# A decoder block with a dense expert stage: more first-layer blocks ahead of it, another DRAM layout for the gates, and a separate place for v's raw buffers

## The chip, the cores and the metric

The kernel runs on one core of one Trainium2 chip, in fp32. The metric is the device time of one execution in microseconds (us), lower is better. The kernel before took 3766.08 us (median of 3 runs, 3752.55 to 3779.93). The profile that is read here is one further execution, of 3775.4 us.

## What is computed

One decoder block over 1024 tokens of width 1024: two gated token mixers (a convolution module and an RWKV-7 scan), then PEER, a mixer that takes 128 experts per token (8 heads, top 16 of each) out of 16384. The change is in the part for PEER, which is in the reference:

```python
e = (i1 * PEER_NKEYS + i2).reshape(TOK_BLOCK, PEER_HEADS * K)      # 128 experts for each token
gate = jax.nn.softmax(best_s, axis=-1).reshape(TOK_BLOCK, PEER_HEADS * K)
u = expert_u[e]
act = jax.nn.gelu(jnp.einsum('td,ted->te', xb, u), approximate=False)
coef = (gate * act.astype(jnp.float32)).astype(xb.dtype)
return jnp.einsum('te,ted->td', coef, expert_v[e])
```

Before it stand the two mixers and the routing (query product and top-k), behind it a norm. None of them is edited.

## The kernel before

The tokens are worked in eight tiles of 128. PEER is done in two ways. Tiles 0, 1 and 2 **gather**: for each of the 128 experts of a token, one indirect DMA (line 1002, issued by POOL) brings 128 rows of 8 KB (the expert's u and v, 1 MB in all) into one of three `row` buffers; VectorE (DVE) takes the dot product with the token (line 1005), ScalarE (ACT) the Gelu and the gate (lines 1006 and 1007), and DVE adds the scaled v to the sum (line 997), which frees the buffer. Tile 0 is gathered before the dense stage, tiles 1 and 2 (256 gathers) beside it, two for each block. Tile 3 takes its activations by gathers ahead of it and the second layer densely.

Tiles 4 to 7 (512 tokens) are **dense**: all 16384 experts, as 128 blocks of 128, are multiplied out, and a gate that is zero for an expert that was not chosen picks the right ones. It has these stages.

- `spread_gates`: for 32 tokens at a time one-hot matrices are built on DVE, ACT and POOL (lines 1073 to 1084), and TensorE (PE) multiplies them (line 1085) into `gt`, whose entry for (expert inside a block, block, token) is the gate. `gt` has two buffers. Each of the 20 pieces goes to DRAM tensor `gd` by one DMA from ACT's queue (line 1089), but for blocks 0 to 7, which stay in two tiles in SBUF (`direct`).
- `u_stage`, the first layer of a block: two loads of 256 KB from `eut` (line 234, SP's queue), split into high and low fp32r parts on ACT and POOL (lines 224 and 225), 24 matmuls of 128x512 (lines 228 to 230), Gelu. It is run ahead of the dense stage for the blocks in `PRE` (56 of 128), and its 256 KB result `g1` is stored in DRAM (`gs`, line 1232) and loaded again (line 1129). These blocks run beside `spread_gates` and the gathers of tile 0.
- `dense`: 32 groups of four blocks. For each group one tile of gates, `gblk` (1.25 MB), is loaded from `gd` (line 1124), in two DMAs; for each block `u_stage` is run if the block is not in `PRE`, the activation is multiplied by the gate (line 1132) and split into `c`; then for each half of v's columns the four blocks' rows of v are loaded (`vraw`, 256 KB each, line 1149, three buffers), split into `vhi` and `vlo`, and 60 matmuls for five token tiles are added up (line 1159). So a group has 120 matmuls of the second layer, and 96 more where its blocks are not in `PRE`.

`PRE` holds every other group, 0, 2, ... 26. Groups 28 to 31 are not in it. These are called PRE groups and full groups below.

The order on each engine is set by a scheduler that works with its own estimate of times, from program order and priorities; on the chip each engine and each DMA queue then runs its instructions strictly in that order. SP issues all loads of the dense stage: an issue that waits holds back those behind it. The pools for `vhi`, `vlo` and `vraw` (`vb`) and for `c` (`cb`) are opened after `spread_gates` has closed its own, and lie where those were.

Of the kernel before, what the change touches and what calls it, by code (L numbers as in the profile page):

```python
# [10 lines left out]
F32 = mybir.dt.float32  # L11
# [9 lines left out]
P = 128  # L21
# [10 lines left out]
GT = 32  # L32
# [3 lines left out]
WD = 512 + XD  # L36
DT = list(range(4, 8)) + list(range(NGT, 4))
NG, NQ, GB, NB = WD // GT, 512 // GT, 4, 4
PRE = [b for b in range(128) if b // 4 % 2 == 0][:56]
NROW = 3  # L40
NV2 = 6
SOONER = 300
# [90 lines left out]
def body(tc, a, out):  # L133
    nc = tc.nc
    V, A, G, PE, SY = nc.vector, nc.scalar, nc.gpsimd, nc.tensor, nc.sync
# [9 lines left out]
    top = ExitStack()  # L145
    cp = pool(top, "cp")
    dr = pool(top, "dr", space=DRAM)
# [40 lines left out]
    zr = [dr.tile([P, 1 + T], F32, name=f"zr{j}") for j in range(14)]  # L188
    hd = [dr.tile([P, D], F32, name=f"hd{j}") for j in range(4)]
    xg = [dr.tile([P, D], F32, name=f"xg{j}") for j in range(4)]  # L190
    gd = dr.tile([NG, P, P, GT], F32, name="gd")
    gs = [dr.tile([P, 512], F32, name=f"gs{b}") for b in range(P)]
    sga = [[dr.tile([P, 512], F32, name=f"sga{j}_{h}") for h in range(2)] for j in range(16)]
    sil = [[dr.tile([P, 512], F32, name=f"sil{j}_{h}") for h in range(2)] for j in range(4)]
# [848 lines left out]
    def spread_gates(es, direct):  # L1043

        gtp = pool(es, "gtp", 2)
        sb = pool(es, "sg_", 2)
        ps_ = pool(es, "sgp", 2, PSUM)
        keys = ps_.tile([P, P], F32, name="keys", bufs=1)
        A.activation(keys, iota, AF.Copy)
        for s_, tt in sorted(enumerate(DT), key=lambda x: x[1]):  # L1050
            hf, tl = divmod(tt, 4)
            src = []
            for k in range(3):
                f = sb.tile([P, P], F32, name="gsrc", tag="gsrc")
                if k < 2:
                    ii = sb.tile([P, P], I32, name="gint", tag="gint")
                    V.tensor_single_scalar(ii, idx[hf][:, tl], 7 if k == 0 else 127,
                                           op=OP.logical_shift_right if k == 0 else OP.bitwise_and)
                    V.tensor_copy(f, ii)
                else:  # L1060
                    f = gate[1][:, tl] if hf else coef[0]
                pt = ps_.tile([P, P], F32, name="gtp")
                PE.transpose(pt, f, ident)
                ft = sb.tile([P, P], F32, name=f"gT{k}")
                A.activation(ft, pt, AF.Copy)
                src.append(ft)
            for g in range(P // GT):
                gt = gtp.tile([P, P, GT], F32, name="gt")
                for q in range(GT // 4):
                    pg = ps_.tile([P, 4, P], F32, name="pg", bufs=3)  # L1070
                    t0 = GT * g + 4 * q
                    o2 = sb.tile([P, 4, P], F32, name="o2h", bufs=3)
                    V.tensor_tensor(o2, src[1][:, t0:t0 + 4, None].to_broadcast([P, 4, P]),
                                    keys[:, None, :].to_broadcast([P, 4, P]), op=OP.is_equal)
                    o1 = sb.tile([P, 4, P], F32, name="o1h", bufs=3)
                    V.tensor_tensor(o1[:, :2], src[0][:, t0:t0 + 2, None].to_broadcast([P, 2, P]),
                                    keys[:, None, :].to_broadcast([P, 2, P]), op=OP.is_equal)
                    for x in range(4):
                        t = t0 + x
                        if x < 2:  # L1080
                            A.activation(o1[:, x], o1[:, x], AF.Copy, scale=src[2][:, t:t + 1])  # L1081
                        else:
                            (V if x == 2 else G).tensor_scalar(o1[:, x], keys if x == 2 else iota, src[0][:, t:t + 1], src[2][:, t:t + 1],
                                                               op0=OP.is_equal, op1=OP.mult)
                        PE.matmul(pg[:, x], o2[:, x], o1[:, x], start=True, stop=True)  # L1085
                    A.activation(gt[:, :, 4 * q:4 * q + 4], pg.rearrange("p t i -> p i t"), AF.Copy)
                for k, d in enumerate(direct):
                    A.activation(d[:, P // GT * s_ + g], gt[:, GB * k:GB * k + GB], AF.Copy)
                A.dma_start(gd[P // GT * s_ + g][:, GB * len(direct):], gt[:, GB * len(direct):])


    def u_stage(b, g1, x2, pu=None):
# [4 lines left out]
        A.activation(pu if g1 is None else g1, pu, AF.Gelu)  # L1097
        return pu

    def dense(es, x2, gp, hr, direct, gk1):  # L1100

        cb = pool(es, "cb")
        rows = gather_rows(gp, range(1, NGT), NROW, {}, pool(es, "rp", 1, PSUM))
        vb = pool(es, "vb", 2, side="right")
# [10 lines left out]
        for g0 in range(0, P, NB):  # L1115
            blks = range(g0, g0 + NB)
            cs = []
            for b in blks:
                if b < GB * len(direct):
                    gtile = direct[b // GB]  # L1120
                elif b % GB == 0:
                    gtile = gk[b // GB % 2].tile([P, NG, GB, GT], F32, name="gblk", tag="gblk")
                    for qs in (slice(0, NQ), slice(NQ, NG)):
                        SY.dma_start(gtile[:, qs].rearrange("p q b t -> p q (b t)"),  # L1124
                                     gd[qs, :, b:b + GB].rearrange("q p b t -> p q (b t)"))
                g1 = up.tile([P, 512], F32, name="g1")
                if b in PRE:
                    act = g1
                    SY.dma_start(g1, gs[b])
                else:  # L1130
                    act = u_stage(b, None, x2, bank())
                V.tensor_mul(g1.rearrange("p (q t) -> p q t", q=NQ), act.rearrange("p (q t) -> p q t", q=NQ), gtile[:, :NQ, b % GB])
                c2 = cb.tile([P, 2, WD], F32R, name="c2", bufs=NB + 1)
                split(c2[:, 0, :512], c2[:, 1, :512], g1)
                split(c2[:, 0, 512:].rearrange("p (q t) -> p q t", t=GT), c2[:, 1, 512:].rearrange("p (q t) -> p q t", t=GT),
                      gtile[:, NQ:, b % GB])
                cs.append(c2)
                if b == NB - 1:
                    for tt in range(NGT, 4):
                        hb[tt] = gp.tile([P, D], F32, name="hr3", tag="hr0")  # L1140
                        SY.dma_start(hb[tt], hd[tt])
                for _ in range(0 if b < NB - 1 else 2 * NB if b == NB - 1 else 2):
                    next(rows, None)
            for n in range(2):
                ns = slice(512 * n, 512 * n + 512)
                vs = []
                for b in blks:
                    raw = vb.tile([P, 512], F32, name="vraw", bufs=3)
                    SY.dma_start(raw, a["euv"][b * P:(b + 1) * P, D + 512 * n:D + 512 * n + 512])
                    hi = vb.tile([P, 512], F32R, name="vhi", bufs=NV2)  # L1150
                    lo = vb.tile([P, 512], F32R, name="vlo", bufs=NV2)
                    split(hi, lo, raw)
                    vs.append((hi, lo))
# [67 lines left out]
    with tc.high_priority(offset=LATER):  # L1221
        gather_coefs(gp, NGT, NEARLY, P)
        for _ in gather_rows(gp, [0], NROW, pace):
            pass
    gk1 = pool(top, "gk1", side="right")
    direct = [p.tile([P, NG, GB, GT], F32, name="gblk", tag=t) for p, t in ((hr, "gblk"), (gk1, "gblk"))]
    with ExitStack() as e0:
        spread_gates(e0, direct)
# [2 lines left out]
        u_stage(b, g1, x2)  # L1231
        SY.dma_start(gs[b], g1)
    with ExitStack() as e0:
        dense(e0, x2, gp, hr, direct, gk1)
    top.close()


# [12 lines left out]
```

## Time and profile before

| what | before |
|---|---|
| median of the runs | 3766.08 us |
| the profiled execution: time / span from first to last instruction | 3775.4 / 3773.6 us |
| mixers and routing | 0 to about 1662 us |
| `u_stage` for PRE, `spread_gates`, gathers of tile 0 | about 1662 to 2290 us |
| dense groups 0 to 31 | 2290 to 3749 us |
| final norm and output | 3749 to 3773.6 us |
| busy: PE / DVE / POOL / ACT | 89% / 72% / 62% / 41% |

Busy time is that of an engine's instructions in the span; a wait belongs to the instruction behind it, and is put down to what ended it. Matmuls overlap, so a busy PE need not be at its peak: the number of matmuls in a stretch and the granted clock (1.0 is 2.4 GHz, 0.5 is 1.2 GHz) tell more. The bounds of groups in the tables below are the ends of their last addition (line 1159).

### The profile page before, as it was taken

The numbers are of one execution on the slowest core, as the hardware profiler recorded it, in microseconds if no ns is written. First come the engines' busy times: TensorE is split into PE (matmuls) and PEld (weight loads), VectorE is DVE, ScalarE is ACT, GpSimd is POOL, SyncE is SP. The second block draws the span as 40 slices with busy tenths as digits, with TensorE's granted clock in tenths as the row PEclk, the third lists the DMA queues.
The fourth block names the chain that finished last, engine by engine and source line by source line (L and its number), as shares of the span: only waits on it lengthen the run. The fifth ranks groups of instructions, "written<-read, shape, count | busy, mean of one in ns | idle before, by whom it ended". The sixth has DMA issues, their size and how long they took to land. (4 is left out here: it accounts for less than half of the span.)

```text
span 3773.6 us, 49258 instructions
## 1 busy us (share of the span) xinstructions
PE 3344.9 (89%) x16175; PEld 2676.8 (71%) x16175; DVE 2720.8 (72%) x5108; ACT 1556.8 (41%) x3712; POOL 2341.3 (62%) x2123
## 2 busy tenths in 40 slices
PE   7999998798889987788899967889898998989997
PEld 7887775586567765666688855777776777767786
DVE  3565449789986768799999996666666566656762
ACT  5555443334443442433366664333333333333343
POOL 3442315446787537656889976666666676666773
PEclk9999989999897878899999988999999999999998
DMA  4321114424677678743799978888888888888991
GB/s 152 104 66 53 49 59 139 139 82 148 208 230 222 202 248 307 265 164 130 250 325 328 330 277 314 310 300 315 301 298 297 285 294 303 299 306 306 330 332 60
DMA packets 343124, 861.36 MB, mean 228 GB/s; under 512 B 53304, under 2 KB 132800, under 8 KB 290900
## 3 DMA queue, kind: packets, MB, share of 16 engines
q0 software_dynamic: 75328, 475.06, 35.3%
q1 hardware_dynamic: 252420, 322.48, 26.6%
q10 hardware_dynamic: 15120, 60.68, 4.1%
q8 instruction: 128, 2.10, 0.2%
q14 instruction: 128, 1.05, 0.1%
HBM read 774.33 MB, written 83.77 MB: 227 GB/s over the span
## 5 line engine op out<-in xcount | busy, mean ns | idle before, releaser
L1002 POOL DMA_INDIRECT row<-euv,idx x384 | 416.9, 1086 | 340.2 <-DVE yr L997 169.2
L225 POOL TENSOR_TENSOR vlo<-vraw,vhi 128x512 fp32r<-128x512 f32 x256 | 328.6, 1297 | 231.5 <-ACT vhi L224 209.8
L997 DVE SCALAR_TENSOR_TENSOR yr<-row,act,yr 128x1024 f32<-128x1024 f32 x256 | 329.3, 1286 | 157.8 <-ACT act L1007 154.7
L1005 DVE SCALAR_TENSOR_TENSOR row<-row,xr 128x1024 f32<-128x1024 f32 x256 | 311.4, 1217 | 175.1 <-DMA row<-euv,idx 167.5
L1006 ACT ACTIVATE act<-act 128x1 f32<-128x1 f32 x384 | 76.8, 200 | 744.9 <-DVE row L1005 744.1
L225 POOL TENSOR_TENSOR ul<-ur,uh 128x512 fp32r<-128x512 f32 x256 | 340.4, 1337 | 38.3 <-ACT uh L224 29.3
L228 PE MATMUL py<-vhi,c 128*128 128x512 f32 x640 | 263.5, 416 | 80.6 <-DVE hbuf L1159 43.2
L230 PE MATMUL zp<-x,ul 128*128 128x512 f32 x736 | 295.3, 402 | 17.5 <-POOL ul L225 17.4
L228 PE MATMUL zp<-x,uh 128*128 128x512 f32 x736 | 295.5, 401 | 0.7 <-ACT g L1097 0.7
L229 PE MATMUL zp<-x,uh 128*128 128x512 f32 x736 | 294.1, 400 | 0.0
L228 PE MATMUL zp<-vhi,c 128*128 128x512 f32 x640 | 255.0, 408 | 34.9 <-DVE hbuf L1159 26.9
L224 ACT ACTIVATE vhi<-vraw 128x512 fp32r<-128x512 f32 x256 | 159.0, 626 | 294.9 <-DMA vraw<-euv 146.8
L230 PE MATMUL py<-vhi,c 128*128 128x512 f32 x640 | 258.9, 411 | 20.6 <-POOL c L225 20.6
L229 PE MATMUL py<-vlo,c 128*128 128x512 f32 x640 | 261.3, 408 | 0.0
L229 PE MATMUL zp<-vlo,c 128*128 128x512 f32 x640 | 253.7, 400 | 0.0
L230 PE MATMUL zp<-vhi,c 128*128 128x512 f32 x640 | 251.7, 401 | 0.0
L997 DVE SCALAR_TENSOR_TENSOR hr<-row,act,hr 128x1024 f32<-128x1024 f32 x128 | 227.4, 1776 | 29.4 <-ACT act L1007 29.2
L349 DVE SCALAR_TENSOR_TENSOR cy<-u,vec,cy 128x512 f32<-128x512 f32 x240 | 242.7, 1011 | 5.4
L1085 PE MATMUL pg<-o1h,o2h 128*128 128x128 f32 x1280 | 186.8, 297 | 50.4 <-ACT o1h L1081 48.0
L1026 DVE SCALAR_TENSOR_TENSOR row<-row,xng 128x1024 f32<-128x1024 f32 x128 | 185.9, 1459 | 58.5 <-DMA row<-euv,twice 58.4
L1024 POOL DMA_INDIRECT row<-euv,twice x128 | 155.2, 1213 | 114.8 <-DVE row L1026 70.0
L1005 DVE SCALAR_TENSOR_TENSOR row<-row,xng 128x1024 f32<-128x1024 f32 x128 | 202.0, 1579 | 33.2 <-DMA row<-euv,idx 33.2
(1646 smaller groups left out, 9516.1 us busy)
## 6 DMA issues: line engine op xcount, KB each, us to landing
ur<-eut SPq DMA_DIRECT2D x256, 256.0 KB, 5.8
vraw<-euv SPq DMA_DIRECT2D x256, 256.0 KB, 5.7
gd<-gt ACTq DMA_DIRECT2D x20, 1920.0 KB, 10.1
gblk<-gd SPq DMA_DIRECT2D x30, 1024.0 KB, 15.9
wbr<-w_in SPq DMA_DIRECT2D x64, 256.0 KB, 3.1
wqr<-w_q SPq DMA_DIRECT2D x64, 256.0 KB, 3.1
wrr<-w_in SPq DMA_DIRECT2D x56, 256.0 KB, 2.9
gs<-g SPq DMA_DIRECT2D x56, 256.0 KB, 4.7
```

The source lines that it names most:

```text
L224: A.activation(hi, src, AF.Copy)
L225: return eng.tensor_sub(lo, src, hi.bitcast(F32))
L228: PE.matmul(ps, whi, xhi, start=first, stop=False)
L229: PE.matmul(ps, whi, xlo, start=False, stop=False)
L230: PE.matmul(ps, wlo, xhi, start=False, stop=last)
L349: V.scalar_tensor_tensor(y, u[:, j:j + 512], cw, y, op0=OP.mult, op1=OP.add)
L997: V.scalar_tensor_tensor(y, row[:, 1], act[:, j:j + 1], y, op0=OP.mult, op1=OP.add)
L1002: G.indirect_dma_start(out=row.rearrange("p a d -> p (a d)"), out_offset=None, in_=a["euv"], in_offset=bass.IndirectOffsetOnAxis(ap=idx[0] ...
L1005: V.scalar_tensor_tensor(row[:, 0], row[:, 0], 1.0, xn, op0=OP.mult, op1=OP.mult, accum_out=aj)
L1024: G.indirect_dma_start(out=row, out_offset=None, in_=a["euv"].rearrange("e (k d) -> (e k) d", k=2), in_offset=bass.IndirectOffsetOnAxis(ap ...
L1026: V.scalar_tensor_tensor(row, row, 1.0, xn, op0=OP.mult, op1=OP.mult, accum_out=act[:, j:j + 1])
L1085: PE.matmul(pg[:, x], o2[:, x], o1[:, x], start=True, stop=True)
```

## The change

There are three edits. `PRE` has 68 blocks: those of all even groups, and blocks 124 to 127, so groups 0, 2, ... 28, 30 and 31. `gd` is laid out by group of four blocks, then partition, then piece: the store of a piece (now line 1090) writes 30 runs of 512 B for each partition, and a `gblk` load is one DMA that reads one run of 10 KB for each partition, where before the store wrote one run of 15 KB and the load read 20 runs of 512 B. `vraw` has a pool of its own (`vr`), opened before `spread_gates`.

```diff
-PRE = [b for b in range(128) if b // 4 % 2 == 0][:56]
+PRE = [b for b in range(128) if b // 4 % 2 == 0 or b >= 120]
...
-    gd = dr.tile([NG, P, P, GT], F32, name="gd")
+    gd = dr.tile([P // GB, P, NG, GB * GT], F32, name="gd")
...
-                A.dma_start(gd[P // GT * s_ + g][:, GB * len(direct):], gt[:, GB * len(direct):])
+                k = len(direct)
+                A.dma_start(gd[k:, :, P // GT * s_ + g].rearrange("k p x -> p k x"), gt[:, GB * k:].rearrange("p (k b) t -> p k (b t)", b=GB))
...
-                    for qs in (slice(0, NQ), slice(NQ, NG)):
-                        SY.dma_start(gtile[:, qs].rearrange("p q b t -> p q (b t)"),
-                                     gd[qs, :, b:b + GB].rearrange("q p b t -> p q (b t)"))
+                    SY.dma_start(gtile.rearrange("p q b t -> p (q b t)"), gd[b // GB].rearrange("p q x -> p (q x)"))
...
-                    raw = vb.tile([P, 512], F32, name="vraw", bufs=3)
+                    raw = vr.tile([P, 512], F32, name="vraw")
...
+    vr = pool(top, "vr", 3, side="right")
```

On SP's queue, the loads of a full group and the PRE group that follows it (g is the stored first layer of a block, ur a half block of `eut`). Before:

```order
L1129 DMA g_24722<-gs_151 128x512
L1124 DMA gblk<-gd 128x16x128
L1124 DMA gblk<-gd 128x4x128
L234 DMA ur<-eut 128x512 x2
L1129 DMA g_24742<-gs_152 128x512
L1129 DMA g_24762<-gs_153 128x512
L1149 DMA vraw<-euv 128x512 x4
L1129 DMA g_24782<-gs_154 128x512
L1149 DMA vraw<-euv 128x512 x3
L1124 DMA gblk<-gd 128x16x128
L1124 DMA gblk<-gd 128x4x128
L1149 DMA vraw<-euv 128x512 x8
```

After the change, the same place:

```order
L1128 DMA g_25192<-gs_151 128x512
L1124 DMA gblk<-gd 128x2560
L234 DMA ur<-eut 128x512 x2
L1128 DMA g_25212<-gs_152 128x512
L1128 DMA g_25232<-gs_153 128x512
L1148 DMA vraw<-euv 128x512 x4
L1128 DMA g_25252<-gs_154 128x512
L1148 DMA vraw<-euv 128x512 x2
L1124 DMA gblk<-gd 128x2560
L1148 DMA vraw<-euv 128x512 x9
```

The order is nearly the same; two DMAs of 2048 and 512 runs have become one of 128 runs, at the same place, with the same loads of `vraw` and g behind it.

On ACT, around the store of the last piece but one of `spread_gates` (o1h and gt belong to it, act to a gather, uh and g to a `u_stage`). Before:

```order
L1086 ACTIVATE gt<-pg 128x128x4 x2
L1006 ACTIVATE act<-act 128x1
L1088 ACTIVATE gblk<-gt 128x128 x2
L1089 DMA gd<-gt 128x3840
L1081 ACTIVATE o1h<-o1h,gT_17161 128x128 x2
L1007 ACTIVATE act<-act,gate_5953 128x1
L1081 ACTIVATE o1h<-o1h,gT_17161 128x128 x2
L1086 ACTIVATE gt<-pg 128x128x4
```

After:

```order
L1081 ACTIVATE o1h<-o1h,gT_17164 128x128 x2
L1088 ACTIVATE gblk<-gt 128x128 x2
L1090 DMA gd<-gt 128x30x128
L1006 ACTIVATE act<-act 128x1
L224 ACTIVATE uh<-ur 128x512
L1007 ACTIVATE act<-act,gate_5953 128x1
L1098 ACTIVATE g_20313<-zp 128x512
L1081 ACTIVATE o1h<-o1h,gT_17164 128x128 x2
L1086 ACTIVATE gt<-pg 128x128x4 x3
```

Before, the last `u_stage` stood at the 15th of the 20 pieces, and the last five pieces had none beside them; now the 12 more blocks stand there, about two to a piece, and the last ends with the last piece.

On POOL, the end of the dense stage (ul belongs to a `u_stage`, c to the activation or the gates). Before:

```order
L1002 DMA row<-euv,idx_5952 128x2048
L225 TENSOR_TENSOR c_30571<-g_30531,c_30571 128x512
L225 TENSOR_TENSOR c_30628<-gblk,c_30628 128x128
L225 TENSOR_TENSOR ul<-ur,uh 128x512 x2
L225 TENSOR_TENSOR c_30628<-g_30588,c_30628 128x512
L225 TENSOR_TENSOR c_30876<-gblk,c_30876 128x128
L225 TENSOR_TENSOR vlo<-vraw,vhi 128x512 x8
```

After:

```order
L1002 DMA row<-euv,idx_5952 128x2048
L225 TENSOR_TENSOR vlo<-vraw,vhi 128x512
L225 TENSOR_TENSOR c_31036<-g_31033,c_31036 128x512
L225 TENSOR_TENSOR c_31036<-gblk,c_31036 128x128
L225 TENSOR_TENSOR vlo<-vraw,vhi 128x512
L225 TENSOR_TENSOR c_31056<-gblk,c_31056 128x128
L225 TENSOR_TENSOR vlo<-vraw,vhi 128x512
L1002 DMA row<-euv,idx_5952 128x2048
L225 TENSOR_TENSOR c_31056<-g_31053,c_31056 128x512
L1002 DMA row<-euv,idx_5952 128x2048
L225 TENSOR_TENSOR vlo<-vraw,vhi 128x512 x3
```

Before, the row of a gather that is shown is the last one of the kernel, and ten `vlo`, more than a whole group's eight, follow it; now groups 30 and 31 have six gathers each, and the last one stands just ahead of the last three `vlo`. By the count of POOL's rows full groups with gathers have 9 to 12 and PRE groups 6 as a rule, in both orders.

## Rows read from the trace of the kernel before

**Rows 1.** Stretches: us, busy us (instructions) of PE, PEld, DVE, ACT, POOL; clock, DMA.

```profile
1900.00:2180.00 280.00, 267.99 (x1560) 231.24 (x1559) 275.58 (x438) 191.64 (x521) 257.51 (x207) 1.00 0.91 329
2180.00:2290.00 110.00, 59.73 (x343) 53.57 (x342) 91.13 (x176) 65.81 (x182) 68.32 (x61) 0.79 0.73 269
2331.30:3548.40 1217.10, 1108.42 (x4587) 883.91 (x4586) 784.98 (x1042) 411.73 (x1052) 818.20 (x767) 0.95 0.86 303
3548.40:3599.60 51.20, 47.74 (x203) 38.85 (x202) 34.60 (x46) 18.69 (x48) 36.85 (x35) 0.97 0.94 334
3599.60:3650.40 50.80, 49.55 (x217) 40.50 (x217) 35.79 (x49) 19.89 (x51) 37.64 (x35) 1.00 0.95 336
3650.40:3699.60 49.20, 49.20 (x217) 40.54 (x216) 32.36 (x42) 22.63 (x51) 31.97 (x29) 1.00 0.64 223
3699.60:3748.90 49.30, 49.30 (x218) 40.60 (x218) 9.50 (x15) 18.05 (x38) 19.07 (x17) 1.00 0.09 28
```

**Rows 2.** One pair of groups, 8 (PRE) and 9 (full), same columns.

```profile
2653.80:2690.50 36.70, 31.05 (x122) 24.00 (x121) 22.32 (x30) 9.18 (x25) 21.75 (x22) 0.92 0.79 267
2690.50:2743.70 53.20, 52.65 (x226) 42.57 (x224) 36.24 (x50) 20.23 (x51) 38.38 (x36) 0.98 0.92 324
```

**Rows 3.** Waits in groups 1 to 27: total us, times, longest us.

```profile
POOL vlo L225 <- ACT vhi L224: 167.7, 50, 11.2
ACT vhi L224 <- DMA vraw<-euv: 133.7, 52, 10.6
DVE g L1132 <- DMA g<-gs: 76.4, 16, 9.3
```

**Rows 4.** Chain of waits, 2653 to 2745 us, its longest pieces: start, us, what.

```profile
2664.24 9.71 SPq L1124
2674.05 9.47 DMA vraw<-euv
...
2725.07 10.88 DMA g<-gs
```

**Rows 5.** Timeline of SP, ACT and PE in that PRE group: start, us; [idle before, ended by].

```profile
2663.82 10.14 SPq L1124 DMA_DIRECT2D gblk<-gd  x2
2683.62 0.63 ACT L224 ACTIVATE vhi<-vraw 128x512 fp32r<-128x512 f32 x1 [7.45 <-DMA vraw<-euv]
2686.40 0.79 PE L228 MATMUL zp<-vhi,c 128*128 128x512 f32 x1 [3.18 <-DVE hbuf L1159]
```

**Rows 6.** Issues of the `gblk` loads and of the stores: ns min/median/max, first to last start.

```profile
L1124 SPq DMA_DIRECT2D gblk<-gd x60: 377/1080/10947, 2306.0 to 3626.6; - x60
L1089 ACTq DMA_DIRECT2D gd<-gt x20: 326/326/361, 1887.5 to 2278.0; - x20
```

**Rows 7.** DMA queues (packets, MB, share of 16 engines): 2306.5-2313.2 us; 1900-2180; groups 1-27.

```profile
q1 hardware_dynamic: 2794, 1.69, 91.8%
...
q10 hardware_dynamic: 1873, 25.56, 22.0%
gd<-gt ACTq DMA_DIRECT2D x13, 1920.0 KB, 9.8
...
gblk<-gd SPq DMA_DIRECT2D x27, 1024.0 KB, 15.7
```

**Rows 8.** Instructions by line, 1900 to 2180 us, then gathers of groups 1 to 27.

```profile
L1085 PE MATMUL pg<-o1h,o2h 128*128 128x128 f32 x843 | 114.9, 283 | 11.9 <-ACT o1h L1081 9.9 <-POOL o1h L1083 1.5
L1086 ACT ACTIVATE gt<-pg 128x512 f32<-128x512 f32 x106 | 60.2, 584 | 5.7 <-PE pg L1085 5.5
...
L1002 POOL DMA_INDIRECT row<-euv,idx x220 | 212.4, 966 | 182.4 <-DVE yr L997 151.3 <-issue 17.6 <-DVE sqf L1039 3.6
```

**Rows 9.** Timeline at the start of the dense stage, ACT and PE, columns as in rows 5.

```profile
2287.78 0.63 ACT L224 ACTIVATE c<-g 128x512 fp32r<-128x512 f32 x1 [1.76 <-DMA gd<-gt]
2298.23 0.63 ACT L224 ACTIVATE vhi<-vraw 128x512 fp32r<-128x512 f32 x1 [1.25 <-DMA vraw<-euv]
2298.92 0.80 PE L228 MATMUL py<-vhi,c 128*128 128x512 f32 x1 [21.56 <-ACT vhi L224]
```

More of the change, by code (lines that the diff above doesn't have):

```diff
@@ L1098, in u_stage, with dense @@
         return pu
-    def dense(es, x2, gp, hr, direct, gk1):
+    def dense(es, x2, gp, hr, direct, gk1, vr):
         cb = pool(es, "cb")
@@ L1233, in body @@
     with ExitStack() as e0:
-        dense(e0, x2, gp, hr, direct, gk1)
+        dense(e0, x2, gp, hr, direct, gk1, vr)
     top.close()
```

## The prediction

> **What bounds the kernel now.** I read the table of stretches first, then the dense stage's waits and its chain, then the timeline at one place of it, then the DMA queues of the stage ahead.
>
> The last two groups set the scale [rows 1]: with no transfers left to wait for, a full group takes 49.2 us at clock 1.0, which for 216 matmuls is 0.228 us each. By that a PRE group (120 matmuls) needs 27.3 us. Groups 1 to 27, 14 full and 13 PRE, would need 14 x 49.2 + 13 x 27.3 = 1044 us; they take 1217.1 [rows 1]. So 173 us, 12.8 for each of 13.5 pairs, are lost, part of it with PE idle, part with the clock at 0.5 after an idle time (mean 0.95). The loss is in the PRE groups: group 8 takes 36.7 us at clock 0.92, the full group behind it 53.2 at 0.98 [rows 2].
>
> What is it? POOL waits 167.7 us for `vhi`, ACT 133.7 us for `vraw`, DVE 76.4 us for `g` [rows 3]: loads come late, though DMA is busy only 0.86 of the stretch [rows 1]. The chain tells why: SP is held 9.71 us at line 1124, then follow 9.47 us for a `vraw` and, in the next group, 10.88 us for a `g` [rows 4]. In group 8 SP issues the two `gblk` loads at 2663.82 and is held for 10.14 us; the `vraw` loads stand behind them, ACT gets the next at 2683.62 after 7.45 us of idleness, and PE resumes at 2686.40 after 3.18 us [rows 5]. An issue of `gblk` takes 0.38 us at best and 10.95 at worst [rows 6]: the first of a pair goes at once, the second waits while the first one's 2048 runs drain.
>
> The stage ahead is bound differently. From 1900 to 2180 us PE is busy 268 of 280 us, DVE 276, DMA 0.91; only ACT has room (192). From 2180 on the first-layer blocks are used up, and PE is busy 60 of 110 us at clock 0.79 [rows 1].
>
> **The change, part by part**, against the profiled execution (3775.4 us, 0.25% above the median).
>
> *Twelve blocks leave groups 28, 30 and 31.* Group 28, now a PRE group with gathers, goes from 51.2 us to the 36.7 of group 8 [rows 1, 2]: -14.5. Groups 30 and 31 go from 49.2 and 49.3 to something between 27.3 (PE alone) and 36.7; they have six gathers each, and group 29 shows that eleven fit into 50.8 us, 4.6 each, so six need 28. I take 33: -32.5. Sum **-47** (bounds -40 and -58).
>
> *They enter the stage ahead.* Twelve blocks are 288 matmuls, 65.7 us. They stand in the last five pieces (2180 to 2278 us), where in the order shown there was none. From 1900 to 2180 PE runs 1560 matmuls, 843 of them of line 1085 [rows 1, 8]; the other 717 are 163 us by 0.228, and the remaining 105 us of busy time give 0.124 us for each of the 843. From 2180 on there are 343 of those [rows 1], 43 us at full clock; with 65.7 that is 108, at the 96% busy that PE reaches before 2180 it is 113 us instead of 98: **+15** (bounds 5 and 25). So of 65.7 us moved, most is filled into PE's idle time.
>
> *`gblk` as one load of 128 runs.* SP's issue becomes one of 128 runs, as the store was with its 0.33 us [rows 6], and the `vraw` and `g` loads behind it go out up to 10 us earlier. What it is worth I read from group 8: 3.18 us idle and 0.08 x 36.7 = 2.9 us for the clock are 6.1 us; times 13.5 pairs **-80**. The bounds are 0 (another wait takes its place) and -173 (the whole loss). Two floors lie below: DMA time in a pair is 0.86 x 90 = 77 us, and the long runs save some. In the one stretch where a `gblk` load has the queue nearly alone, 2794 packets take 0.918 x 16 x 6.7 = 98 us of one engine, 35 ns each; 2560 of 512 B are 5.6 us of all 16, against 3.2 for the same 1.31 MB at the rate of the long stores (0.220 x 16 x 280 us for 25.56 MB) [rows 7]. So DMA needs 72 us of a pair, the gathers (220 in 13.5 pairs [rows 8], 16.3 each) 16.3 x 4.6 = 75, and the pair comes to 84. After that the gathers are late next: POOL already waits 151.3 us for a free row buffer [rows 8].
>
> *The stores in 512 B runs.* Each of the 20 stores has 3840 runs instead of 128. A store now costs 0.220 x 16 x 280 / 13 = 76 us of one engine, 4.7 of all [rows 7]; at 35 ns a run it is 8.4. So up to 3.7 us more for each piece of 21.5 us (280 / 13), 74 in all, in a stage whose DMA is busy 0.91. The bounds are 0 and +75. DVE and PE bind there and loads are prefetched, so I take a fifth: **+15**. The Trainium skill (DMA: Bandwidth & Descriptors, Specifications) gives 512 B as the least size that still moves at line rate; by that the stores cost nothing more, and the sum would be 15 us lower. The trace disagrees in part: at 0.918 busy the short runs moved 1.69 MB in 6.7 us, 253 GB/s, against 329 GB/s over the stage at 0.91 [rows 1, 7].
>
> ACT issues these stores, and its queue is strict: behind a held store stand o1h (PE waits for it) and gt. The issue takes 0.33 us now [rows 6]. I cost it at nothing, because an issue of 2048 runs with nothing ahead of it goes out as fast as one of 128 (0.38 and 0.33 us at best [rows 6]), and the next DMA on ACT's queue comes 20 us later. If that is wrong it is the first rival.
>
> A store must also land before its `gt` buffer is written again, one piece later. It lands in 9.8 us and ACT never waits for it there [rows 7, 8]; the larger part of a `gblk` load, 2048 short runs, lands in 15.7 us beside gathers [rows 7]. That is close, but fits.
>
> *`vraw` in a place of its own.* Before, `c` and `vhi` wait for the last store (2287.78), then `vraw` is loaded, and `vhi` starts at 2298.23; PE is idle 21.56 us [rows 9]. Three early loads save those 10 us; the last store, landing perhaps 6 us later, takes most back: **-4** (bounds -10 and +5).
>
> *The end.* The last gather now stands ahead of the last three `vlo`, so tile 2's norm and output fall into the final norm: **+5** (bounds 0 and 15).
>
> Sum: -47 + 15 - 80 + 15 - 4 + 5 = **-96**: 3679 us for a profiled execution, **3670** against the median.
>
> **Rivals.**
>
> 1. *ACT is held by the stores (slower).* If a store holds ACT's queue as the second `gblk` holds SP's, 9.7 us each [rows 4], 20 of them hold it 194 us. ACT is busy 192 of 280 us [rows 1], 14.7 of a piece of 21.5, so at least 14.7 + 9.7 - 21.5 = 2.9 us for each piece come out, 58 in all; at most all 194, since PE waits for ACT's o1h there. The middle, 126, gives 3670 + 126 = 3796, slower than before. It decides from 96 / 20 = 4.8 us of exposed hold for each store. For it: SP is held so. Against: there it is the second DMA that is held, and ACT has none. Chance 0.12.
>
> 2. *The DMA engines bind the stage ahead.* The small packets have changed their queue and not vanished; 0.91 x 21.5 = 19.6 us of DMA in a piece become 23.3, which at the 0.95 of group 29 [rows 1] take 24.5; the piece grows by 3 us and the stage by 60 instead of 15: 3715; with the dense gain at 50 instead of 80, 3745. Against: the short runs would have to reach the upper bound, and from 2180 on DMA is busy only 0.73 [rows 1]. The Trainium skill (DMA: Bandwidth & Descriptors, Issuing engines are not separate DMA queues) says that DMAs from all engines run on the same 16 and interleave, so that another issuing queue saves only issue time; by that rule this rival is the stronger, and what the dense stage's DMA is relieved of would come back here. Chance 0.17.
>
> 3. *The gathers bind the dense stage.* Three row buffers, a landing, two passes on DVE and POOL's strict queue give one row in 4.6 us at best and 5.5 in a mean pair; if that can't be hurried, earlier `vraw` loads only move the wait to POOL's line 1002, and the groups keep their times. The gain of 80 shrinks to 10: 3740. For it: POOL's 151.3 us of waiting. Against: group 29's eleven in 50.8 us. Chance 0.15.
>
> **Numbers.** The forecast has 0.56, with a range of its own of 3610 to 3725 (the dense gain between 40 and 130, the stores between 0 and 30). About 1% (38 us) is what a measurement of this kernel can tell from no change: faster means below 3728, slower above 3804. Faster: all of the forecast, half of rival 2, a fifth of rival 3, 0.56 + 0.09 + 0.03 = 0.68. Slower: two thirds of rival 1, 0.08. Within 1%: the rest, 0.24. For 8 in 10 the range takes in most of rivals 2 and 3 and leaves out rival 1 and the far end of the gain: 3612 to 3755.
>
> **What would show it.** In the changed kernel's profile: issues of `gblk` at 0.33 to 1 us; ACT's wait for `vraw` and POOL's for `vhi` less than half of before; PRE groups of about 31 us; groups 30 and 31 of about 33 us; the stage ahead ending near 2320 us, PE busy up to its end; issues of the store on ACT at 0.33 to 0.5 us, landing in 15 to 20. The prediction is wrong if the store's issue takes several us (rival 1), if ACT's gt (line 1086) waits for the store or the stage ends after 2360 (rival 2), or if pairs still take 88 to 90 us while POOL waits longer for row buffers (rival 3).

## The result, and the profile after

The changed kernel takes **3655.4 us** (median of 4 runs, 3652.0 to 3670.3) against 3773.0 of the kernel before on the same chip (4 runs, 3752.6 to 3787.3): a ratio of **0.971**, 95% interval 0.967 to 0.975. Forecast were 3670 us and a range of 3612 to 3755. The profiled execution has a span of 3668.5 us against 3773.6, 105.1 less.

Stretches of the kernel after, columns as in rows 1. The first two are the stage ahead, the third groups 1 to 27, the next four groups 28 to 31, the last two the pair 8 and 9.

```profile
1900.00:2180.00 280.00, 271.10 (x1577) 233.83 (x1576) 275.61 (x434) 191.10 (x519) 257.50 (x206) 1.00 0.99 329
2180.00:2305.00 125.00, 105.91 (x624) 92.47 (x622) 114.11 (x186) 86.98 (x227) 106.36 (x88) 0.94 1.00 329
2345.90:3499.60 1153.70, 1080.54 (x4581) 868.70 (x4580) 785.08 (x1047) 413.88 (x1055) 819.82 (x768) 0.97 0.88 320
3499.60:3530.60 31.00, 28.87 (x124) 22.72 (x124) 21.43 (x30) 9.66 (x26) 21.76 (x22) 1.00 0.88 307
3530.60:3582.10 51.50, 49.73 (x212) 40.48 (x211) 40.19 (x54) 18.37 (x49) 35.62 (x34) 0.97 0.91 340
3582.10:3613.10 31.00, 28.32 (x122) 22.30 (x121) 25.99 (x35) 11.03 (x31) 23.32 (x23) 1.00 0.89 299
3613.10:3642.70 29.60, 28.05 (x122) 22.39 (x121) 22.00 (x28) 16.01 (x43) 15.90 (x15) 1.00 0.63 227
2656.50:2693.10 36.60, 29.30 (x113) 22.74 (x112) 21.68 (x29) 9.52 (x27) 22.37 (x23) 0.86 0.83 293
2693.10:2743.60 50.50, 48.65 (x212) 39.44 (x211) 35.03 (x48) 18.86 (x49) 37.58 (x35) 1.00 0.89 318
```

| part of the span | before | after | difference | forecast |
|---|---|---|---|---|
| up to the end of group 0 | 2331.3 | 2345.9 | +14.6 | +26 (15 + 15 - 4) |
| groups 1 to 27 | 1217.1 | 1153.7 | -63.4 | -80 |
| groups 28 to 31 | 200.5 | 143.1 | -57.4 | -47 |
| behind the last group | 24.7 | 25.8 | +1.1 | +5 |
| sum | 3773.6 | 3668.5 | -105.1 | -96 |

The waits of groups 1 to 27 (total us, times, longest), against rows 3 and the 151.3 us of rows 8:

```profile
POOL row L1002 <- DVE yr L997: 143.1, 61, 7.1
POOL vlo L225 <- ACT vhi L224: 116.9, 56, 7.4
ACT vhi L224 <- DMA vraw<-euv: 79.4, 43, 8.0
DVE g L1131 <- DMA g<-gs: 46.8, 16, 5.6
```

The issues of the `gblk` load and of the store, against rows 6:

```profile
L1124 SPq DMA_DIRECT2D gblk<-gd x30: 326/327/617, 2320.2 to 3556.7; - x30
L1090 ACTq DMA_DIRECT2D gd<-gt x20: 366/366/428, 1889.8 to 2292.8; - x20
```

SP is no longer held: a `gblk` issue took 10.95 us at worst and now takes 0.62, and the issue behind the load ends 2.4 us after the load's began (mean over 30), where before it was 8.6. A store's issue on ACT takes 0.43 us at most, and the next store is the next issue there, so the 3840 runs hold nothing on that queue. The loads that stood behind `gblk` are waited for less in sum. No time went over to the row buffers (143.1 us against 151.3). The start of the dense stage, columns as in rows 5, against rows 9:

```profile
2292.79 0.37 ACTq L1090 DMA_DIRECT2D gd<-gt  x1
...
2311.53 0.63 ACT L224 ACTIVATE c<-g 128x512 fp32r<-128x512 f32 x1 [7.77 <-DMA gd<-gt]
...
2313.13 0.79 PE L228 MATMUL py<-vhi,c 128*128 128x512 f32 x1 [21.40 <-ACT vhi L224]
```

ACT now waits 7.77 us for the last store where it was 1.76: that store lands 18.7 us after its issue (2292.79 to 2311.5), before 9.8. PE's gap is the old one, 21.40 us.

### The profile page after: what moved, and what is told of

Same layout as the page of the kernel before. It is cut to its first block, busy times and chain, and to the rows that moved or that the text cites. A ratio compares the mean times of both kernels' runs of the same rounds, so it can differ in the third digit from the quotient of the medians.

```text
span 3668.5 us, 49271 instructions
## 1 busy us (share of the span) xinstructions
PE 3313.7 (90%) x16175; PEld 2656.0 (72%) x16175; DVE 2738.7 (75%) x5108; ACT 1554.1 (42%) x3711; POOL 2344.6 (64%) x2123
## 5 line engine op out<-in xcount | busy, mean ns | idle before, releaser
L225 POOL TENSOR_TENSOR ul<-ur,uh 128x512 fp32r<-128x512 f32 x256 | 344.7, 1353 | 36.4 <-ACT uh L224 27.3
L230 PE MATMUL zp<-x,ul 128*128 128x512 f32 x784 | 314.3, 401 | 16.9 <-POOL ul L225 16.9
L228 PE MATMUL py<-vhi,c 128*128 128x512 f32 x640 | 258.9, 409 | 68.2 <-DVE hbuf L1158 31.6
L228 PE MATMUL zp<-x,uh 128*128 128x512 f32 x784 | 314.9, 402 | 0.3 <-ACT g L1098 0.3
L229 PE MATMUL zp<-x,uh 128*128 128x512 f32 x784 | 313.7, 400 | 0.0
L230 PE MATMUL py<-vhi,c 128*128 128x512 f32 x640 | 254.0, 403 | 23.5 <-POOL c L225 23.5
L228 PE MATMUL zp<-vhi,c 128*128 128x512 f32 x640 | 249.5, 399 | 12.0 <-DVE hbuf L1158 10.1
L997 DVE SCALAR_TENSOR_TENSOR hr<-row,act,hr 128x1024 f32<-128x1024 f32 x128 | 235.1, 1837 | 33.8 <-ACT act L1007 33.5
L230 PE MATMUL zp<-vhi,c 128*128 128x512 f32 x640 | 246.8, 395 | 0.0
L1005 DVE SCALAR_TENSOR_TENSOR row<-row,xng 128x1024 f32<-128x1024 f32 x128 | 213.7, 1672 | 16.0 <-DMA row<-euv,idx 16.0
L1026 DVE SCALAR_TENSOR_TENSOR row<-row,xng 128x1024 f32<-128x1024 f32 x128 | 184.3, 1445 | 51.9 <-DMA row<-euv,twice 51.7
L228 PEld LDWEIGHTS py<-vhi,c 128*128 128x128 f32 x640 | 124.0, 194 | 110.1 <-DVE hbuf L1158 43.2
```

The source lines that it names most:

```text
L225: return eng.tensor_sub(lo, src, hi.bitcast(F32))
L228: PE.matmul(ps, whi, xhi, start=first, stop=False)
L229: PE.matmul(ps, whi, xlo, start=False, stop=False)
L230: PE.matmul(ps, wlo, xhi, start=False, stop=last)
L997: V.scalar_tensor_tensor(y, row[:, 1], act[:, j:j + 1], y, op0=OP.mult, op1=OP.add)
L1005: V.scalar_tensor_tensor(row[:, 0], row[:, 0], 1.0, xn, op0=OP.mult, op1=OP.mult, accum_out=aj)
```

## The experiments

Each has its edit against the kernel after or before, as named. Kernels were run on three chips beside the kernel before (medians there 3767.1 to 3778.5 us), so they are compared by ratio. Two numbers stand for each: the ratio of the whole time, and groups 1 to 27 of its profile. To see how far a single profile can be trusted, the kernel before was profiled a second time:

> The kernel before once more, for a second profile: how far the ends of its stages move from one execution to the next. Theory: groups 1 to 27 within 8 us of 1217, groups 28 to 31 within 2 us of 200.5; the first store of the gates within 15 us of 1887.5. If the stretch 1 to 27 moves by more than 15 us, the splits by single profiles are worth less than the medians.

It took 3775.45 us; groups 1 to 27 took 1207.6 us against 1217.1, and the first store went out at 1895.4 against 1887.5. So a profile's groups 1 to 27 carry some 10 us of chance, and the stages ahead of the first store, which the edits hardly touch, moved between 1859 and 1896 us from kernel to kernel. Two profiles lie well below their kernel's median, mostly by that: e3_vr's (3728.0 us, median 3751.4) and f3_layout_short's (3717.9, median 3741.6), in which the first store went out 27 and 29 us earlier than before.

| kernel | `gblk` load: runs, apart in DRAM, queue | PRE | groups 1 to 27 | ratio (95%) |
|---|---|---|---|---|
| before | 2 DMAs, 512 B, 2 MB, SP | 56 | 1217.1, 1207.6 | 1 |
| e6_one_short_sp | 1 DMA, 512 B, 2 MB, SP | 56 | 1216.3 | 1.0027 (1.0001 to 1.0053) |
| f3_layout_short | 512 B, 768 B, SP | 56 | 1189.2 | 0.9932 (0.9905 to 0.9959) |
| e2_layout | 10 KB, SP | 56 | 1163.7 | 0.9841 (0.9799 to 0.9883) |
| f2_before_act | 512 B, 2 MB, ACT | 56 | 1140.7 | 0.9844 (0.9800 to 0.9889) |
| e5_short_loads | 512 B, 768 B, SP | 68 | 1181.2 | 0.9774 (0.9758 to 0.9791) |
| after | 10 KB, SP | 68 | 1153.7 | 0.9710 (0.9671 to 0.9750) |
| f1_long_act | 10 KB, ACT | 68 | 1157.6 | 0.9747 (0.9697 to 0.9798) |
| f4_old_layout_act | 512 B, 2 MB, ACT | 68 | 1143.7 | 0.9716 (0.9672 to 0.9760) |
| **e7_short_act** | 512 B, 768 B, ACT | 68 | **1112.9** | **0.9604** (0.9548 to 0.9660) |

Apart: the distance between a partition's runs. The rows with 68 also have the place of `vraw`.

### The three edits one by one

**e1_pre68**, the kernel before with one line:

```diff
-PRE = [b for b in range(128) if b // 4 % 2 == 0][:56]
+PRE = [b for b in range(128) if b // 4 % 2 == 0 or b >= 120]
```

> The kernel before with the first edit alone: 68 blocks ahead instead of 56, gates' layout and vraw as before. Theory (three separate gains): groups 28 to 31 go from 200.5 us to about 36.5 + 51 + 2 x 33 = 154 (two of them keep the held loads, so more than the changed kernel's 143), the stage ahead ends 12 to 15 us later; 30 to 35 us faster than before, ratio about 0.991. The start of group 0 against that of the changed kernel also shows what the 512 B stores cost there: theory 0 to 15 us. Rival (work is only moved from one stage to the other): ratio 1.00.

Measured: 3737.5 us, 0.9907 (0.9876 to 0.9938). Its groups 28 to 31, as a stretch:

```profile
3554.00:3711.40 157.40, 139.80 (x566) 110.54 (x565) 112.41 (x148) 54.88 (x145) 96.06 (x92) 0.93 0.79 274
```

That is 43.1 us less than the 200.5 before; groups 1 to 27 did not move (1216.5), and from the first store to PE's first matmul of the dense stage it took 424.8 us against 411.4. Term 1 (-47) and term 2 (+15) hold by themselves.

**e2_layout**, the kernel before with the layout of `gd`, the store and the single load of the change.

> The kernel before with the gates' layout alone (stores in 512 B runs, one long load for each group). Theory: groups 1 to 27 go from 1217 us to about 1150, as in the changed kernel; groups 28 to 31 stay near 200; the stage ahead is 0 to 15 us longer by the stores; 55 to 65 us faster, ratio about 0.984. Rival (the dense gain of the changed kernel comes from vraw's place or from the other order of the schedule): groups 1 to 27 stay above 1195 and the ratio is within 0.5% of 1.

Measured: 3725.2 us, 0.9841 (0.9799 to 0.9883). Groups 28 to 31, full here, took 208.3 us, 7.8 more than before; groups 1 to 27:

```profile
2334.60:3498.30 1163.70, 1082.56 (x4574) 869.64 (x4573) 780.44 (x1043) 413.31 (x1053) 819.20 (x766) 0.97 0.87 317
```

53.4 us less than before, and the 20 stores in short runs cost the stage ahead nothing: first to last store 387.3 us against 390.5. Only the last one's late landing shows: from its issue to PE's first dense matmul 25.8 us instead of 20.9.

**e3_vr**, the kernel before with `vraw` in its own pool.

> The kernel before with vraw's own place alone. Theory: PE's idle time at the start of the dense stage goes from 21.6 to about 11 us, as vhi then waits only for the last store (which lands 9 us after its issue here), and nothing else moves: 5 to 12 us faster, ratio 0.997 to 0.999. Rival (c and vhi wait for the store, and vraw's load was hidden): 0. Second rival (vraw's place is what shortens the groups): groups 1 to 27 near 1150.

Measured: 3751.4 us, 0.9937 (0.9920 to 0.9953): 24 us, against 4 in the prediction. In its profile PE's gap ahead of the dense stage is 14.2 us instead of 21.6:

```profile
2251.78 0.79 PE L228 MATMUL py<-vhi,c 128*128 128x512 f32 x1 [14.16 <-ACT vhi L224]
```

First to last store took 377.6 us instead of 390.5. The first is what the edit does. The other 13 us I can't tie to it: its stretch ahead was also scheduled differently. The gain is measured, its larger half is not explained.

The three losses of ratio, 0.0093, 0.0159 and 0.0063, add up to 0.0315; the whole change gave 0.029. So the parts are additive within their intervals.

### What of the layout does it: the DMA count, the place, the run length

Theory A: what counts is how long the runs hold SP's queue. The rival, B: it is where the runs lie in DRAM, or that two DMAs became one. **e6_one_short_sp** changes the count alone, in the kernel before:

```diff
-                    for qs in (slice(0, NQ), slice(NQ, NG)):
-                        SY.dma_start(gtile[:, qs].rearrange("p q b t -> p q (b t)"),
-                                     gd[qs, :, b:b + GB].rearrange("q p b t -> p q (b t)"))
+                    SY.dma_start(gtile.rearrange("p q b t -> p q (b t)"), gd[:, :, b:b + GB].rearrange("q p b t -> p q (b t)"))
```

> The kernel before, layout as before (runs of 512 B in a load), but each gblk load is one DMA of 2560 runs on SP's queue in place of two. The run with short loads in the changed kernel took back only 27 of the 63 us that groups 1 to 27 had gained, so the rest must come from the number of DMAs with the order that follows from it, or from the runs' place in DRAM. Theory A (one DMA and its order): groups 1 to 27 near 1185 us, ratio about 0.990 to 0.993; SP's hold still 8 us, now behind the next vraw. Theory B (runs 2 MB apart in DRAM are what was slow): groups 1 to 27 stay at 1205 to 1217, ratio 0.998 to 1.002.

Measured: 3778.0 us, 1.0027 (1.0001 to 1.0053). One issue instead of two gives nothing. Its groups 1 to 27 and its issues:

```profile
2327.90:3544.20 1216.30, 1104.58 (x4580) 882.04 (x4579) 785.60 (x1042) 412.56 (x1052) 817.40 (x767) 0.95 0.87 303
```

```profile
L1123 SPq DMA_DIRECT2D gblk<-gd x30: 377/377/812, 2301.1 to 3624.8; - x30
```

The issue itself is as short as after the change. The hold has only moved to the next issue on SP, whose end comes 9.3 us after that of `gblk` began (mean over 30; 8.6 before, behind both DMAs, 2.4 after the change).

**e5_short_loads** is the kernel after with runs of 512 B: 256 B of padding behind each, so that they can't be joined. Every other instruction stands in the same order.

```diff
-    gd = dr.tile([P // GB, P, NG, GB * GT], F32, name="gd")
+    gd = dr.tile([P // GB, P, NG, GB * GT + 64], F32, name="gd")
...
-                    SY.dma_start(gtile.rearrange("p q b t -> p (q b t)"), gd[b // GB].rearrange("p q x -> p (q x)"))
+                    SY.dma_start(gtile.rearrange("p q b t -> p q (b t)"), gd[b // GB, :, :, :GB * GT])
```

> The changed kernel, but with 256 B of padding behind each 512 B run of the gates in DRAM, so that a gblk load (one DMA) reads 20 runs of 512 B for each partition again; the stores keep their 512 B runs, PRE and vraw are as changed. Theory (short runs hold SP's queue and delay vraw and g): groups 1 to 27 go back to about 1200 to 1217 us, the stage ahead stays as in the changed kernel; 55 to 75 us slower than the changed kernel, about 3715 to 3730, ratio to the kernel before 0.985 to 0.99. Rival (the gain comes from the number of DMAs, the order or vraw's place, not from the runs' length): as the changed kernel, 0.971.

Measured: 3692.1 us, 0.9774 (0.9758 to 0.9791). The whole hold is back (next issue over 8.5 us after), yet groups 1 to 27 lose only 27.5 us of 63.4. **f3_layout_short** does the same to e2_layout:

> The layout alone with padding (one DMA of short runs per gblk on SP's queue, PRE and vraw as before): against the run with one DMA of short runs in the old layout (1216 us for groups 1 to 27) it differs in where the runs lie in DRAM, 768 B apart in place of 2 MB, with almost the same order. The short loads in the changed kernel had 1181. Theory A (the place in DRAM makes the difference): 1180 to 1190, ratio 0.990 to 0.993. Theory B (vraw's place or the order with 68 blocks does): 1205 to 1217, ratio 0.998 to 1.003.

Measured: 3741.6 us, 0.9932 (0.9905 to 0.9959). Groups 1 to 27 of e5 and of f3:

```profile
2324.60:3505.80 1181.20, 1097.23 (x4591) 876.64 (x4589) 782.92 (x1047) 413.00 (x1059) 817.92 (x768) 0.97 0.89 313
```

```profile
2301.00:3490.20 1189.20, 1099.83 (x4580) 881.38 (x4579) 781.79 (x1043) 412.16 (x1052) 817.22 (x767) 0.96 0.89 310
```

The kernels e6, f3 and e2 run the same instructions in the same order on ACT, DVE, POOL and SP. So the layout's gain has two halves. From 2 MB between a partition's runs to 768 B (e6 to f3): 27.1 us, ratio 0.0095. From 512 B to 10 KB (f3 to e2): 25.5 us, ratio 0.0091. Theory A holds for the second half, B for the first: the place, not the number of DMAs. Why the place matters is open.

### Another queue for the load

If what stands behind `gblk` on SP is the cost, ACT's queue should free it. **e7_short_act** is e5 with the load issued by ACT:

```diff
-                    SY.dma_start(gtile.rearrange("p q b t -> p q (b t)"), gd[b // GB, :, :, :GB * GT])
+                    A.dma_start(gtile.rearrange("p q b t -> p q (b t)"), gd[b // GB, :, :, :GB * GT])
```

> The changed kernel with short runs in the gblk loads, as in the run with short loads, but these loads are issued from ACT's queue, where no other DMA stands in the dense stage. Theory (it is SP's hold that costs, not the transfer of short runs): SP issues vraw and g without a hold, ACT is not held, groups 1 to 27 come within 10 us of the changed kernel's 1154, ratio to the kernel before about 0.972. Rival (the transfer itself, 16 us to land instead of 9 and more DMA time, delays vraw and g whichever queue issues it): as with short loads on SP, 1181 us and 0.977. Second rival (ACT is held and its queue passes the hold on): slower than 0.985.

Measured: **3623.5 us, 0.9604 (0.9548 to 0.9660)**, faster than both kernels, and than the theory, which had the changed kernel's time. Groups 1 to 27:

```profile
2343.00:3455.90 1112.90, 1069.51 (x4578) 864.00 (x4576) 783.33 (x1046) 416.59 (x1053) 820.21 (x768) 0.99 0.94 332
```

PE's clock is 0.99 and its idle time 43 us, against 0.97 and 73 after the change. By that, long runs from ACT should be better still; **f1_long_act** is the kernel after with `A.dma_start` at line 1124, its instructions in e7's order:

> The changed kernel with its gblk loads (long runs, one DMA) issued from ACT's queue in place of SP's. The order on all engines is that of the run with short runs on ACT, so the two differ in the runs' length alone, as the changed kernel and the run with short loads do on SP. Theory (what costs is what stands behind gblk on SP's queue): the length matters little on a queue of its own; groups 1 to 27 within 15 us of the 1113 of that run, ratio 0.956 to 0.961. Rival (DMA time binds now, at 0.944 busy): the long runs give 25 to 35 us more, groups 1 to 27 at 1080 to 1088, ratio 0.950.

Measured: 3679.9 us, 0.9747 (0.9697 to 0.9798): a miss. Groups 1 to 27:

```profile
2342.40:3500.00 1157.60, 1084.52 (x4577) 874.39 (x4576) 782.45 (x1046) 413.88 (x1051) 819.29 (x767) 0.96 0.88 319
```

45 us more than e7, with only the runs different. Where: PE has 16 gaps of 2 us or more, of which 11 end 9 to 14 us after an issue of `gblk`; e7 has 8 gaps, one of them there. The DMA queues (packets, MB, share of 16 engines) in the 8 us that begin 2 us after the `gblk` issue of one full group, first f1 then e7. Queue 0 holds the gathers, 1 SP's loads, 10 ACT's:

```profile
q0 software_dynamic: 202, 1.52, 45.5%
q10 hardware_dynamic: 139, 1.28, 42.5%
q1 hardware_dynamic: 170, 0.32, 10.9%
```

```profile
q0 software_dynamic: 211, 1.52, 47.4%
q1 hardware_dynamic: 389, 0.72, 26.2%
q10 hardware_dynamic: 1155, 0.59, 25.8%
```

With long runs the three queues move similar numbers of packets, and the one with 10 KB packets takes 1.28 MB while SP's 2 KB packets get 0.32. With short runs SP gets 0.72 MB in the same time. Over all 27 loads the same windows give SP 0.43 and 0.62 MB. The `gblk` load lands after 10.7 us in f1 and 22.6 in e7, and no engine is seen waiting for it in either kernel's groups 1 to 27. Of SP's loads in these groups whose landing is recorded, those issued in the 8 us behind a `gblk` issue landed after 11.1 us in f1 (median of 18) and 9.3 in e7 (of 25), the others after 5.7 and 5.9. The Trainium skill (DMA: Bandwidth & Descriptors, Queues, rings and completion order) says that each DMA engine takes turns between the queues packet by packet, a packet being several descriptors. f1's near-equal counts agree with such turns; e7's 211, 389 and 1155 don't by themselves, and no run here shows how the profile's packets relate to the page's. That the longer runs cost these 45 us is shown, since only the padding differs. That the crowding makes the late gaps fits these rows; it is not shown, since no experiment with other packet sizes for `vraw` was run, and in sum `vraw` and `g` are waited for as long in e7 as in f1 (108.0 and 107.1 us).

Two more kernels have short runs on ACT's queue at the old place in DRAM: **f2_before_act**, the kernel before with one load of 2560 runs from ACT, and **f4_old_layout_act**, which adds the 68 blocks and the place of `vraw`.

> The kernel before (its layout, PRE and vraw) with one edit: each gblk load is one DMA of short runs from ACT's queue. Theory (the queue is the cause): groups 1 to 27 near 1115 to 1130 us, 85 to 100 us faster than the kernel before, ratio 0.974 to 0.978, more than the layout alone gave (0.984). Rival (the runs' length or place in DRAM is the cause, and the queue helped only in the new layout): groups 1 to 27 above 1165, ratio above 0.985.

> The kernel before with 68 blocks ahead, vraw's own place and gblk as one DMA of short runs from ACT's queue: the changed kernel without its layout, with the queue in its place. Theory: groups 1 to 27 near 1113 us, as with the padded layout on ACT; the last store of the gates lands about 6 us earlier after its issue; ratio 0.957 to 0.961, so the layout is not needed once the queue is another. Rival (2 MB apart is slow on any queue): groups 1 to 27 above 1135 us, ratio above 0.966.

Measured: 3710.3 us, 0.9844 (0.9800 to 0.9889), between its theory and its rival, and 3660.8 us, 0.9716 (0.9672 to 0.9760), the rival's case. Groups 1 to 27:

```profile
2332.00:3472.70 1140.70, 1073.58 (x4573) 865.13 (x4572) 782.33 (x1042) 412.98 (x1051) 818.10 (x766) 0.98 0.92 323
```

```profile
2329.80:3473.50 1143.70, 1083.45 (x4584) 872.24 (x4583) 787.75 (x1046) 414.52 (x1055) 819.61 (x768) 0.97 0.92 323
```

Against e6 the other queue is worth 76 us in groups 1 to 27 and 0.0183 of the ratio: as much as the whole new layout on SP's queue (0.0159). With the queue the scheduler also moved other instructions, so these are the worth of queue and order together, as the 68 us from e5 to e7 are; that the order is not the cause by itself is seen from f1, which has e7's order and is no faster than the kernel after. And the place in DRAM is worth as much here as on SP: 1143.7 (f4) against 1112.9 (e7), in the same order of instructions on ACT, DVE, POOL and SP, ratio 0.0112. The Trainium skill (DMA: Bandwidth & Descriptors, Latency and other measured facts) reports slower copies where the rows of neighbouring partitions lie 2 MB or more apart. Here it is a partition's own runs that lie 2 MB apart and the partitions 16 KB, so the direction agrees, and the page's case is another.

### Mixed groups

**e8_mixed** asks if the alternation of PRE and full groups is what the loads can't follow: two blocks of every group are stored ones.

```diff
-PRE = [b for b in range(128) if b // 4 % 2 == 0 or b >= 120]
+PRE = [b for b in range(128) if b % 4 < 2 or b >= 120]
```

> The changed kernel with the same number of blocks ahead (68), but two of each group's four in groups 0 to 29, and all of groups 30 and 31. So each group has 168 matmuls (38.3 us at 0.228) instead of 120 and 216 in turn, and each loads about the same bytes. Theory (PRE groups lose time because their loads come faster than their matmuls can cover; full groups have cover to spare): groups 1 to 27 go from 1154 to 27 x 39.5 = 1070 to 1120 us, 30 to 80 us faster than the changed kernel, ratio to the kernel before 0.950 to 0.965. Rival (the loss is in the gathers and POOL's order, evenly spread): 1140 to 1160, ratio 0.97.

Measured: 3663.7 us, 0.9716 (0.9660 to 0.9772), the same as the kernel after: the theory (0.950 to 0.965) missed. Groups 28 to 31, and what is behind them:

```profile
3475.50:3616.40 140.90, 135.01 (x575) 108.38 (x574) 113.34 (x147) 53.22 (x145) 99.67 (x95) 0.99 0.90 321
3616.40:3660.90 44.50, 2.01 (x9) 1.31 (x7) 26.81 (x37) 16.16 (x35) 12.45 (x8) 0.57 0.64 244
```

The waits of groups 1 to 27:

```profile
POOL row L1002 <- DVE yr L997: 233.9, 86, 8.4
DVE g L1131 <- DMA g<-gs: 99.2, 27, 7.7
ACT vhi L224 <- DMA vraw<-euv: 48.6, 41, 2.7
POOL vlo L225 <- ACT vhi L224: 20.9, 27, 2.3
```

Groups 1 to 27 took 1125.5 us, 28.2 less than after, of which some 11 us are 48 matmuls (at 0.228 us) that group 0 now has. `vraw` and `vhi` are waited for less than after (48.6 and 20.9 us against 79.4 and 116.9), `g` more, and POOL waited 233.9 us for row buffers (after: 143.1). Six gathers are issued behind the last group, where the kernel after has none, and what is behind it takes 44.5 us instead of 25.8, in which PE works 2. That is what rival 3 describes, one step further on. How much of it is the gathers' pace and how much the place that the scheduler gave the last six was not tested.

## Why the prediction was right, and where its steps were not

*Twelve blocks leave the end: -47; measured -57.* Alone (e1) -43.1. Together with the layout another 14: groups 28, 30 and 31 took 31.0, 31.0 and 29.6 us, where I had taken 36.7, 33 and 33. The 36.7 was group 8's time of before, with SP's hold in it [rows 2]; I counted the removal of that hold in groups 1 to 27 alone. With the hold back (e5) the four groups took 151.4; but with short runs on ACT's queue, where SP is free, they took 149.4 (e7), so the hold on SP is not shown to be the whole of it.

*Twelve blocks in the stage ahead: +15; measured +13.4 (e1).* The way of filling PE's idle 50 us of rows 1 was right: from 2180 to 2305 us PE is busy 105.9 of 125 at clock 0.94 (59.7 of 110 at 0.79 before).

*One long load: -80; measured -63.4 in groups 1 to 27 (-53.4 alone).* The mechanism was half of it. The waits fell to 0.59 (`vraw`), 0.70 (`vhi`) and 0.61 (`g`) of before, and not below half; PRE groups took 33.7 us in the mean (36.4 before), not 31, and full ones 51.1 (53.2). The step that failed is the reading of the whole gain from group 8. The pair 8 and 9 went from 89.9 to 87.1 us, not to 84, and group 8 itself stayed at 36.6, at clock 0.86; the gain is spread over other pairs and over the full groups, which have 29 of the 63.4 us (14 x 2.1), where I had put the whole loss in the PRE groups. And the run length, to which I gave all of it, brought 25 to 28 us (e2 against f3, after against e5); the other half came from the place in DRAM, of which the prediction says nothing. What is left after the change (PE idle for 73 us) is not a hold of 9 us any more; that the load's own 1.25 MB crowd those beside it fits f1 against e7 on ACT's queue, and on SP's queue it was not tested.

*Stores in 512 B runs: +15; measured nothing in the stage, about 5 us at its end.* From the first store to the last it took 403.0 us, in e1, with the same blocks and the old stores, 406.4. The DMA queues of 1900 to 2180 us show where the term went; ACT's queue, which holds the stores, after (rows 7 have before):

```profile
q10 hardware_dynamic: 50550, 25.78, 31.4%
```

The same 25.6 MB take 31.4% of the 16 engines' time instead of 22.0%: 0.094 x 280 / 13 = 2.0 us for each piece, where I had bounded it at 3.7: a run of 512 B took 27.9 ns of an engine in the mean, and I had put it at 35, from a stretch that held other packets too. DMA rose from 0.91 to 0.99 busy, at an unchanged 329 GB/s, and PE made as many matmuls (1577 against 1560). DMA time was there to be had, as I argued; a fifth of the upper bound was still too much. **Rival 2** (DMA binds the stage) was right that the engines would be nearly full, and wrong on the time. The Trainium skill (DMA: Bandwidth & Descriptors, Issuing engines are not separate DMA queues) has one set of engines under all queues, with which the share agrees, and leaves to another queue only the issue time that it saves, usually small beside the DMA. Here it was not small: e5 to e7 gave 0.0170 of the ratio, 68 us in 27 groups, while the issue of such a load takes 0.53 us (e5).

*The store's issue: nothing; measured 0.37 us, 0.43 at most.* **Rival 1** needed 4.8 us for each store; it is refuted, since each store's issue is the next one on ACT's queue behind the store before it.

*`vraw`'s place and the last store: -4.* In the whole change PE's gap stayed (21.40 us against 21.56), since the store landed later, as I said: with the late store and without the own place it is 26.5 (e2, f3). So the edit saves 5 us there, and the store takes 5. Alone, without the late store, the edit gave 24 us by the medians, of which PE's gap shows 7; the rest is open (e3).

**Rival 3** (gathers bind): pairs take 85 us in the mean (33.7 + 51.1), and POOL waits no longer than before. Not here; in e8 the waits for row buffers grow.

*The end: +5; measured +1.1.* Together: the start was costed 11 us too high, the dense groups 17 too well, the end 10 us too little and the tail 4 too high. These errors nearly cancel, which is why 3670 came within 15 us of 3655. The direction was right, and the mechanisms in the main; so close a number was luck.

## What to carry to other kernels

A load of many short runs costs what stands behind it on its queue: look first at which queue it is issued from, since here moving it to another gave more (0.0170 to 0.0183 of the time) than making its runs longer (0.0064 to 0.0091). A load that nothing waits for soon can stay in short runs on a queue of its own: in this kernel that was faster than long runs there (0.9604 against 0.9747). And a gain per group should be read from the mean of its kind, not from one group with a clear story.

## What the runs showed of the hardware beyond that

- The length of an issue does not show the hold: an issue of 2560 runs takes 0.38 us, and it is the next issue on the same queue that ends 9.3 us after its start (e6); behind 128 runs of 10 KB it is 2.4 us (after).
- A long-run load on a second queue is no gain over the same load on SP's (f1 1157.6 us, after 1153.7), while short runs there gain 68 us (e5 1181.2, e7 1112.9).
- Runs of 512 B that lie 768 B apart, not 2 MB, are worth 27 us in groups 1 to 27 on SP's queue (e6 to f3) and 31 on ACT's (f4 to e7). Why is open: no run varied the distance in steps.
- For the same 25.6 MB, stores in runs of 512 B took 31.4% of the DMA engines' time, in runs of 15 KB 22.0% (1900 to 2180 us, after and before).
